# Start addresses of the large tiles in a decoder layer: multiples of 128 bytes, weight parts 64 bytes behind one

## The chip, the cores and the metric

One Trainium2 chip, of which the kernel uses one core. The metric is the device time of one execution in microseconds (us), the median of several runs. Lower is better.

## What is computed

One layer of a decoder over 256 tokens of width 1024, in float32, batch 1. Three steps add to the residual `x`, and a last RMSNorm follows.

```python
h = rmsnorm(x, norm_mix_g)
x = x + concat(conv_group(h), attention_group(h), gla_group(h)) @ w_out   # groups read columns of h @ w_in
h = rmsnorm(x, norm_xattn_g)
x = x + memory_cross_attention(h, rmsnorm(mem, norm_mem_g), wq, wkv, wo)  # 4 heads, 256 memory tokens
h = rmsnorm(x, norm_ffn_g)
u = causal_dwconv(h @ w_up)                                               # width 3, 2 x 2752 channels
a, g = split(u)
x = x + (silu(a) * g) @ w_down
return rmsnorm(x, final_norm_g)
```

The products must have nearly float32 precision. The kernel gets it from three products in the type float32r: a matrix is split into a high part (its rounding to float32r) and a low part (what is left), and high times high, high times low and low times high are summed in PSUM.

## The kernel before

**Weights.** All weights come from HBM as one stream of pieces of 128 x 1024 float32 (512 KB; some are narrower), in the order of `_stream_order`. `emit_load` (L112) lets SyncE fetch a piece into one of 6 raw tiles. `emit_split` (L128) makes the two parts of it: ScalarE copies the piece into `hi` as float32r (L152), and VectorE subtracts, `lo = raw - hi` (L159). Each part has a pool of 4 slots of 1024 elements (tags `high` and `low`, L146 and L147). Four pieces go to tiles that are idle at the time instead: the two of `wo` to the slot with tag `big`, the two of `up` pair 0 to the slot with tag `parts` (`SPARE`, L49, L136 to L141). `piece` (L164) keeps loads 6 and splits 2 or more pieces ahead of their use.

**Activations.** The moving side of most products is a normed and split activation: `xg` (tag `xg`), `y` (tag `parts`), `memg` and `hn` (tag `hn`), each 16 blocks of 128 x 256, 8 for the high and 8 for the low part. The FFN's hidden values (`hid`, 128 x 256 blocks for high and low of each of 21 channel groups and a tail) take the same three slots again, 16 blocks in each: first `big`, then `parts`, then `xg` (L779 to L782).

**Products and the order on TensorE.** A product with 256 moving columns holds a 128 x 128 block of weights as its stationary side and streams 256 tokens: `first` (L279, 144 matmuls), `in`, `xk`, `xq` and `up` (`feature_tile`, L203 to L212), `out` (`products`, L201), `wo` (L760), and `up` pair 0 (L850). In four places the weights are the moving side and a 128 x 128 block of activations is stationary: `gv` (L442, 272 columns), `v` (L458, 512 columns), `xv` (L718, 256 columns) and the down-projection `dn` (L887, L891, 512 columns, whose stationary side is `hid`). TensorE goes through these one after the other in the written order: `first`; `in` mixed with `gv`, `v` and the small products of the attention and gated groups; `xk`; `out`; `xq`, `xv` and the cross-attention; `wo`; `up` for pairs 0 to 20 and a tail; `dn`. Pairs 0 to 2 of `up` read `xg` and are scaled afterwards, later ones read `hn`, which GpSimd, ScalarE and VectorE make while pairs 1 and 2 run (L861, L187, L190). VectorE and ScalarE do the convolution and the gate of a pair (`activate`, L812) while TensorE is on the next.

**Where a tile starts.** A pool hands out bytes in the order in which its tags are first used, each rounded up to 32 bytes per partition. What starts behind a small or odd-sized tile (the residual with its 8 gains in front, `par` with 213 columns, `eps`, `one`, `lr1`) therefore starts at a multiple of 32, and not always of 128. The start of a slot modulo 128 bytes, as the built program has it:

| slot | holds | before | changed |
|---|---|---|---|
| `res` (2) | residual `x`, `x1`, `x2` | 0 and 32 (the values of `x` 32 further) | 0 and 0 (the values of `x` 0) |
| `big` | attention inputs, parts of `wo`, `hid` of groups 0 to 7 | 64 | 0 |
| `parts` | `y`, parts of `up` pair 0, `hid` of groups 8 to 15 | 0 | 0 |
| `xg` | `xg`, `hid` of groups 16 to 20 and the tail | 96 | 0 |
| `hn` | `memg`, `hn`, final output | 0 | 0 |
| `keep` | row norms | 96 | 0 |
| `high`, `low` (4 each), part used as stationary | weights of `first`, `in`, `xk`, `out`, `xq`, `up` | 0 | 64 |
| `high`, `low`, part used as moving | weights of `gv`, `v`, `xv`, `dn` | 0 | 0 |
| `big`, parts of `wo` | stationary | 64 | 64 |
| `parts`, parts of `up` pair 0 | stationary | 0 | 64 |

Blocks inside these tiles lie 512 or 1024 bytes apart, so a whole product has one pair of starts modulo 128 (`gv` has two: its weight blocks are 1088 bytes apart).

Of the kernel before, what the change touches and what calls it, by code (L numbers as in the profile page):

```python
# [10 lines left out]
F32 = mybir.dt.float32  # L11
BF16 = mybir.dt.bfloat16
F32R = mybir.dt.float32r
# [6 lines left out]
P = 128  # L20
T = 256
D = 1024
KT = D // P
# [13 lines left out]

PG_X, PG_MEM, PG_FFN = 0, 8, 16
P_SCW, P_SCB, P_GN, P_FW, P_FB = 32, 38, 40, 41, 170
NPARAM = 213  # L40

RAW, PARTS, AHEAD = 6, 4, 2
EARLY, STATS, MIXED, TURNED = 3, (1, 0), 1, 3
# [4 lines left out]

SPARE = {("wo", 0): "big", ("wo", 1): "big", ("up", 0, 0): "parts", ("up", 0, 1): "parts"}  # L49
SLOT = 1024  # L50

X_WITH = {1: (1, 2), 2: (2, 4), 4: (4, 8)}

# [16 lines left out]
def _width(key):  # L70
    return {"first": 768, "gla": 544}.get(key[0], 1024)
# [3 lines left out]
def trunk(ctx: ExitStack, tc: tile.TileContext, xT, x_rows, w_stream, params, gate, final, out):  # L75
# [3 lines left out]
    cp = ctx.enter_context(tc.tile_pool(name="cp", bufs=1))  # L79
    rp = ctx.enter_context(tc.tile_pool(name="rp", bufs=RAW))  # L80
    hp = ctx.enter_context(tc.tile_pool(name="hp", bufs=PARTS))
    t1p = ctx.enter_context(tc.tile_pool(name="t1p", bufs=16))
    t2p = ctx.enter_context(tc.tile_pool(name="t2p", bufs=11))
    smp = ctx.enter_context(tc.tile_pool(name="smp", bufs=12))
# [3 lines left out]
    def ps(name):  # L88
        banks["turn"] += 1
        return pp.tile([P, 512], F32, tag=banks["tags"][banks["turn"] % len(banks["tags"])], name=name)  # L90
# [4 lines left out]
    def t2(name):  # L95
        return t2p.tile([P, 2, T], F32, tag="t2", name=name)
# [8 lines left out]
    spare = {}  # L105
    state = {"load": 0, "split": 0, "until": place[("up", 0, 0)]}

    def load_x(k0, k1):
        a, b = (KT + k0 * T if k0 else 0), KT + k1 * T
        sp.dma_start(xt[:, a:b], xT[:, a:b])  # L110

    def emit_load():  # L112
        i = state["load"]
        state["load"] += 1
        key = order[i]
        t = rp.tile([P, SLOT], F32, tag="raw", name="w_" + "_".join(map(str, key)))
        if i == 0:

            act.dma_start(t[:, :384], w_stream[i, :, :384])
            load_x(0, 1)  # L120
            sp.dma_start(t[:, 384:768], w_stream[i, :, 384:768])
        else:
            if key[0] == "first" and key[1] in X_WITH:
                load_x(*X_WITH[key[1]])
            sp.dma_start(t[:, :_width(key)], w_stream[i, :, :_width(key)])
        raw[key] = t

    def emit_split(pin=False):  # L128
        i = state["split"]
        state["split"] += 1  # L130
        key = order[i]
        if key[0] == "mem":
            return
        n = _width(key)
        t = raw[key]
        if key in SPARE:  # L136
            tag = SPARE[key]
            if key[-1] == 0:
                spare[tag] = cp.tile([P, 16, T], F32R, tag=tag, name="spare_" + tag)
            view = lambda c: spare[tag][:, 8 * key[-1] + c:8 * key[-1] + c + 4, :].rearrange("p a b -> p (a b)")  # L140
            hi, lo = view(0), view(4)  # L141
        elif key[0] == "dtail":
            hi = cp.tile([P, n], F32R, name="h_dtail")
            lo = cp.tile([P, n], F32R, name="l_dtail")
        else:
            hi = hp.tile([P, SLOT], F32R, tag="high", name="h_" + "_".join(map(str, key)))[:, :n]  # L146
            lo = hp.tile([P, SLOT], F32R, tag="low", name="l_" + "_".join(map(str, key)))[:, :n]  # L147
        if i == 0:
            act.copy(hi[:, :384], t[:, :384])
            dve.tensor_copy(hi[:, 384:], t[:, 384:n])  # L150
        else:
            c = act.copy(hi, t[:, :n])  # L152
            if pin:
                tc.keep_in_program_order(c)
        if key[0] == "dtail":
            pool.memset(lo[TAIL:].bitcast(F32), 0.0)
            c = dve.tensor_sub(lo[:TAIL], t[:TAIL, :n], hi[:TAIL])
        else:
            c = dve.tensor_sub(lo, t[:, :n], hi)  # L159
        if pin:  # L160
            tc.keep_in_program_order(c)
        parts[key] = (hi, lo)
# [29 lines left out]
    def pair(t, n):  # L192

        return t[:, 0:n, :], t[:, n:2 * n, :]
# [16 lines left out]
            s, m = term(k)  # L211
            pe.matmul(dst, s[a], m[b], start=(n == 0), stop=(n == len(todo) - 1))  # L212

    xt = cp.tile([P, KT + KT * T], F32, tag="res", bufs=2, name="x")
    x = xt[:, KT:].rearrange("p (k n) -> p k n", k=KT)
    emit_load()
    act.preload_act_table_set("natural_log_exp_and_others")
    for _ in range(RAW - 1):
# [5 lines left out]
    for _ in range(KT - RAW):  # L224
        emit_load()
    par = cp.tile([P, NPARAM], F32, name="par")
    sp.dma_start(par, params)
# [6 lines left out]
    dve.memset(heat, 0.0)  # L234
    ones = cp.tile([P, P], F32, name="ones")
    dve.memset(ones, 1.0 / D)
    eps = cp.tile([P, 1], F32, name="eps")
    dve.memset(eps, EPS)
    one = cp.tile([P, 1], F32, name="one")
    dve.memset(one, 1.0)  # L240


# [87 lines left out]
    pool.memset(same, 0.0)  # L330
    for h in range(4):
        pool.memset(same[32 * h:32 * h + 32, 64 * (h % 2):64 * (h % 2) + 64], 1.0)
    lr1 = cp.tile([P, 2, 17], F32, name="lr1")
    pool.memset(lr1, 1.0)
    big = cp.tile([P, 16, T], F32, tag="big", name="mix")
    yt = cp.tile([P, 2 * KT, T], F32R, tag="parts", name="y")
# [81 lines left out]

    mgt = cp.tile([P, 2 * KT, T], F32R, tag="hn", name="memg")
    mg = pair(mgt, KT)  # L420
    macc = cp.tile([P, T], F32, name="m_acc")

    def memory(i):
        m = piece("mem", i)[:, :1024].rearrange("p (k n) -> p k n", k=4)
# [7 lines left out]


    gv = t2("gv")
    lrT = cp.tile([17, T], F32, name="lrT")
    gps = [ps("gv0"), ps("gv1")]
    for i in range(4):
        w = blocks(piece("gla", i), 272)
# [115 lines left out]
    for n, dst in ((0, ue[:, 0:P]), (2, ue[:, P:T]), (1, uo[:, 0:P])):  # L554
        a = 64 * (n % 2)
# [18 lines left out]
    for j in range(2):  # L574
        for h in range(4):
            a = 64 * (h % 2)
# [23 lines left out]
    for c in range(2):  # L600
# [9 lines left out]
        f = t1(f"yg{c}")  # L610
# [119 lines left out]
    for c in range(2):  # L730
        o = ps(f"xo{c}")
        for m in range(2):
            for h in (2 * c, 2 * c + 1):
                a = 64 * (h % 2)
# [93 lines left out]
    def second_root():  # L828
        spread(r2, diags2, "x2")

    r2, ready = smp.tile([P, T], F32, tag="r2", bufs=1, name="r2"), []
    for j in range(NPAIR + 1):
        tail = j == NPAIR
        src = []
        for t in range(1 if tail else 2):
# [6 lines left out]
            elif t == 1:  # L842
# [13 lines left out]
                _, diags2 = root_of(tot2, "x2")  # L856
                tc.keep_in_program_order(act.preload_act_table_set("silu_and_others"))
            if (j, t) == STATS:
                for k in range(KT):
                    f = t1(f"hn{k}")  # L860
# [5 lines left out]
        if j >= STATS[0]:  # L866
            for args in ready:
                activate(*args)
            ready = []
# [29 lines left out]
    k0 = NPAIR - LEAD  # L899
# [35 lines left out]
def _layout(inp):  # L935
    f = lambda n: np.asarray(inp[n], np.float32)
    actT = lambda a: _rows(a[0].T, KT).reshape(P, KT * T)
# [6 lines left out]
    down = w_down[:NPAIR * P].reshape(NPAIR, P, 2, 512).transpose(1, 2, 0, 3).reshape(P, 21, 1024)  # L944

    order = _stream_order()
    stream = np.zeros((len(order), P, SLOT), np.float32)
    for i, key in enumerate(order):
        kind, n = key[0], key[1] if len(key) > 1 else 0
        if kind == "first":  # L950
            a = w_first[n]
        elif kind == "in":
            a = _tile(w_in, n)
        elif kind == "mem":
            a = memT[:, 1024 * n:1024 * n + 1024]
        elif kind == "gla":
            a = _rows(w_gla[256 * n:256 * n + 256], 2)
        elif kind == "mv":
            a = _rows(w_in[256 * n:256 * n + 256, MV:MV + 512], 2)
        elif kind == "out":  # L960
            a = _tile(w_out, n * P)
        elif kind == "wq":
            a = _tile(wq, n * P)
        elif kind == "memk":
            a = _tile(wkv, n * P)
        elif kind == "memv":
            a = _rows(wkv[512 * n:512 * n + 512, 256:], 4)
        elif kind == "wo":
            a = wo.reshape(2, P, KT, P).transpose(1, 2, 0, 3)[:, 4 * n:4 * n + 4]
        elif kind == "up":  # L970
            a = _tile(w_up, n * P + key[2] * DFF)
        elif kind == "uptail":
            a = _tile(tail, 0)
        elif kind == "dtail":
            a = np.concatenate([w_down[NPAIR * P:]] * 2, 0)
        else:
            a = down[:, n]
        a = a.reshape(a.shape[0], -1)
        stream[i, :a.shape[0], :a.shape[1]] = a

    par = np.zeros((P, NPARAM), np.float32)
    for at, n in ((PG_X, "norm_xattn_g"), (PG_MEM, "norm_mem_g"), (PG_FFN, "norm_ffn_g")):
# [7 lines left out]
    for j in range(NPAIR + 1):  # L990
# [4 lines left out]
        for t, c in enumerate(chans):  # L995
            n = 2 * j + t
            par[:, P_FW + 3 * n:P_FW + 3 * n + 3] = cw[:, c].T
            par[:, P_FB + n] = cb[c]
    gate = np.concatenate([f("gla_w_gate")[0], f("gla_b_gate")], 0)
    xT = np.concatenate([f("norm_mix_g").reshape(KT, P).T, actT(f("x"))], 1)  # L1000
    final = np.tile(f("final_norm_g").reshape(1, D), (P, 1))
    return [np.ascontiguousarray(xT), np.ascontiguousarray(f("x")[0]), stream, par, np.ascontiguousarray(gate), final]

# [19 lines left out]
```

## Time and profile before

| what | value |
|---|---|
| median of 3 runs (lowest, highest) | 342.38 us (342.32, 342.47) |
| the profiled execution's own time | 342.1 us |
| its span, first to last instruction | 340.4 us |
| matmuls in the span | 2462 |
| TensorE busy | 331.5 us, 97% |
| TensorE weight loads busy | 306.6 us, 90% |
| VectorE, ScalarE busy | 258.0 us (76%), 210.8 us (62%) |
| mean granted clock of TensorE | 0.997 |

The span lies inside the profiled execution's time, which is 1.7 us longer; that execution is 0.3 us under the median. Busy time of an engine counts the stretches in which at least one of its instructions runs. Matmuls overlap in their pipeline, so how fast a product goes is read from the distance of the starts of its matmuls, not from the duration of one.

### The profile page before, as it was taken

The page shows a single profiled execution, that of the slowest core. Times are in us where ns is not written, and L with a number is a line of the kernel's source. Part 1 is how long each engine was busy: PE and PEld are TensorE (multiplying, and loading weights), DVE is VectorE, ACT ScalarE, POOL GpSimd, SP SyncE. Part 2 cuts the span into 40 slices and gives each one's busy share as a digit, 9 for nine tenths or more (in the row PEclk, how much of TensorE's full clock was granted, in tenths as well). Part 3 has the DMA queues.
Part 4 walks back from the last instruction along what each step waited for, and adds up shares of the span by engine and source line. Part 5 has one row for each costly group of instructions (what it writes and reads, how often), then busy time and mean ns, then how long its engine had stood idle before and what let it go on. Part 6 is the DMA issues. An engine that isn't in the chain of part 4 may idle for free.

```text
span 340.4 us, 6402 instructions
## 1 busy us (share of the span) xinstructions
PE 331.5 (97%) x2462; PEld 306.6 (90%) x2462; DVE 258.0 (76%) x486; ACT 210.8 (62%) x390; POOL 13.3 (4%) x32
## 2 busy tenths in 40 slices
PE   6999999999999999999999999999999999999992
PEld 3999879898999999899899999999999988888881
DVE  5978878797987858578999988888889874454411
ACT  3574999566666655586786666666667654353333
POOL 6000000000000000005400000000000000000000
PEclk9999999999999999999999999999999999999998
DMA  7989753743377534108238765555557546563003
GB/s 211 417 309 324 255 179 103 236 157 129 122 247 249 183 126 129 59 13 287 71 125 244 234 203 188 186 182 182 183 174 241 185 154 194 196 188 104 0 0 123
DMA packets 17888, 60.37 MB, mean 177 GB/s; under 512 B 1969, under 2 KB 2626, under 8 KB 17858
## 3 DMA queue, kind: packets, MB, share of 16 engines
q1 hardware_dynamic: 17426, 59.24, 52.1%
q10 hardware_dynamic: 432, 0.72, 0.6%
q8 instruction: 19, 0.31, 0.4%
q14 instruction: 11, 0.09, 0.1%
HBM read 58.91 MB, written 1.05 MB: 176 GB/s over the span
## 4 chain that ended last, share of the span: by engine, by line
PE 93%; ACT 3%; DVE 2%; DMA 1%; issue 0%; DVEq 0%
PE up L212 35%; PE dn L887 17%; PE in L212 10%; PE out L201 7%; PE first L279 5%; PE v L458 3%; PE gv L442 2%; PE xq L212 2%; PE xv L718 2%; PE wo L760 2%; PE xk L212 2%; ACT h_up L152 1%; DMA x<-in_xT_dram 1%; PE et L385 1%; ACT x_sq L752 1%; PE o L395 1%
## 5 line engine op out<-in xcount | busy, mean ns | idle before, releaser
L212 PE MATMUL up<-hn,h_up 128*128 128x256 f32 x576 | 76.6, 284 | 0.1
L212 PEld LDWEIGHTS up<-hn,h_up 128*128 128x128 f32 x576 | 72.1, 192 | 1.2 <-ACT hn L187 0.9
L152 ACT CAST h_up<-w_up 128x1024 fp32r<-128x1024 f32 x40 | 41.7, 1047 | 24.2 <-PE up L212 24.2
L159 DVE TENSOR_TENSOR l_up<-w_up,h_up 128x1024 fp32r<-128x1024 f32 x40 | 48.7, 1221 | 8.8 <-ACT h_up L152 8.7
L887 PE MATMUL dn<-h_down,hid 128*128 128x512 f32 x168 | 52.7, 392 | 0.0
L159 DVE TENSOR_TENSOR l_down<-w_down,h_down 128x1024 fp32r<-128x1024 f32 x21 | 25.7, 1226 | 25.9 <-ACT h_down L152 25.9
L212 PE MATMUL up<-hn,l_up 128*128 128x256 f32 x288 | 40.4, 283 | 0.0
L152 ACT CAST h_down<-w_down 128x1024 fp32r<-128x1024 f32 x21 | 22.1, 1051 | 29.1 <-PE dn L887 24.9
L887 PEld LDWEIGHTS dn<-h_down,hid 128*128 128x128 f32 x168 | 31.6, 188 | 6.9
L212 PEld LDWEIGHTS up<-hn,l_up 128*128 128x128 f32 x288 | 37.1, 192 | 0.0
L791 DVE SCALAR_TENSOR_TENSOR u<-up,par,u 128x255 f32<-128x255 f32 x74 | 35.1, 477 | 0.6
L887 PE MATMUL dn<-l_down,hid 128*128 128x512 f32 x84 | 32.9, 392 | 0.0
L212 PE MATMUL in<-xg,h_in 128*128 128x256 f32 x192 | 25.8, 286 | 0.0
L212 PEld LDWEIGHTS in<-xg,h_in 128*128 128x128 f32 x192 | 23.8, 188 | 0.7 <-issue 0.5
L789 ACT ACTIVATE u<-up,par 128x256 f32<-128x256 f32 x37 | 20.5, 555 | 0.0
L887 PEld LDWEIGHTS dn<-l_down,hid 128*128 128x128 f32 x84 | 15.8, 188 | 3.5
L201 PE MATMUL out<-y,h_out 128*128 128x256 f32 x128 | 16.7, 283 | 0.0
L201 PEld LDWEIGHTS out<-y,h_out 128*128 128x128 f32 x128 | 15.9, 192 | 0.0
L159 DVE TENSOR_TENSOR l_in<-w_in,h_in 128x1024 fp32r<-128x1024 f32 x12 | 14.6, 1220 | 1.0 <-ACT h_in L152 0.6
L152 ACT CAST h_in<-w_in 128x1024 fp32r<-128x1024 f32 x12 | 12.5, 1047 | 4.3 <-issue 2.8
L279 PE MATMUL first<-xg,h_first 128*128 128x256 f32 x96 | 13.2, 284 | 0.9 <-DVE h_first L150 0.5
L861 POOL TENSOR_TENSOR hn<-x,r 128x256 f32<-128x256 f32 x8 | 7.7, 1002 | 149.8 <-DVE r L313 149.8
(270 smaller groups left out, 561.1 us busy)
## 6 DMA issues: line engine op xcount, KB each, us to landing
w_up<-in_w_stream_dram SPq DMA_DIRECT2D x42, 512.0 KB, 3.4
w_down<-in_w_stream_dram SPq DMA_DIRECT2D x21, 512.0 KB, 3.3
w_in<-in_w_stream_dram SPq DMA_DIRECT2D x12, 512.0 KB, 4.4
w_out<-in_w_stream_dram SPq DMA_DIRECT2D x8, 512.0 KB, 3.4
w_first<-in_w_stream_dram SPq DMA_DIRECT2D x7, 384.0 KB, 8.1
w_mv<-in_w_stream_dram SPq DMA_DIRECT2D x4, 512.0 KB, 4.3
w_gla<-in_w_stream_dram SPq DMA_DIRECT2D x4, 272.0 KB, 4.1
xtok<-in_x_rows_dram SPq DMA_DIRECT2D x1, 1024.0 KB, 9.7
```

What stands on the lines that cost most here:

```text
L152: c = act.copy(hi, t[:, :n])
L159: c = dve.tensor_sub(lo, t[:, :n], hi)
L201: pe.matmul(dst, s, m, start=(n == 0), stop=(n == len(todo) - 1))
L212: pe.matmul(dst, s[a], m[b], start=(n == 0), stop=(n == len(todo) - 1))
L279: pe.matmul(fps[i][:, :T], w[a][:, i * P:(i + 1) * P], xg[b][:, k, :], start=(k == 0 and (a, b) == (0, 0)), stop=(k == KT - 1 and a == 1))
L442: pe.matmul(gps[j][:, :272], xg[a][:, 2 * i + k, j * P:(j + 1) * P], w[b][:, k, :], start=(i == 0 and k == 0 and (a, b) == (0, 0)), stop=( ...
L458: pe.matmul(vps[j], xg[a][:, 2 * i + k, j * P:(j + 1) * P], w[b][:, k, :], start=(i == 0 and k == 0 and (a, b) == (0, 0)), stop=(i == 3 an ...
L718: pe.matmul(vps[j][:, :T], mg[a][:, 4 * i + k, j * P:(j + 1) * P], w[b][:, k, :], start=(i == 0 and k == 0 and (a, b) == (0, 0)), stop=(i ...
L789: act.activation(v, src, AF.Identity, bias=fb(t), scale=fw(t, 2))
L791: dve.scalar_tensor_tensor(v[:, s:], src[:, :T - s], fw(t, 2 - s), v[:, s:], op0=ALU.mult, op1=ALU.add)
L861: pool.tensor_mul(f, x2[:, k, :], r2)
L887: pe.matmul(q, hid[i](k)[:, cols], w[j], start=False, stop=(k == NPAIR - 1 and i == 1), skip_group_check=True)
```

## The change

Nothing is added to or taken from what the engines compute. What changes is where tiles start:

- Tiles ahead of a large one are padded: the gains in front of `x` from 8 to 32 columns, `par` from 213 to 224, `eps` and `one` from 1 to 32, the last axis of `lr1` from 17 to 32. The inputs in HBM are padded alike, so the first transfer of `x` has 288 columns and not 264.
- A weight part that will be stationary begins `ASIDE` = 16 elements (64 bytes) into its slot, which is 32 elements longer; one that will be moving (`MOVING`) begins at the slot's start. The spare slots do the same.
- `m_acc`, `lrT` and `r2` (the row norm of the FFN) share one slot of 256 columns (tag `row`), which makes room for the padding.

```diff
-NPARAM = 213
+NPARAM = 224
...
+ASIDE = 16
+MOVING = ("gla", "mv", "memv", "down", "dtail")
+
+PADDED = 32
...
     def load_x(k0, k1):
-        a, b = (KT + k0 * T if k0 else 0), KT + k1 * T
+        a, b = (PADDED + k0 * T if k0 else 0), PADDED + k1 * T
         sp.dma_start(xt[:, a:b], xT[:, a:b])
...
             if key[-1] == 0:
-                spare[tag] = cp.tile([P, 16, T], F32R, tag=tag, name="spare_" + tag)
-            view = lambda c: spare[tag][:, 8 * key[-1] + c:8 * key[-1] + c + 4, :].rearrange("p a b -> p (a b)")
-            hi, lo = view(0), view(4)
+                spare[tag] = cp.tile([P, 4 * SLOT + 32], F32R, tag=tag, name="spare_" + tag)
+            view = lambda c: spare[tag][:, ASIDE + c * SLOT:ASIDE + (c + 1) * SLOT]
+            hi, lo = view(2 * key[-1]), view(2 * key[-1] + 1)
...
-            hi = hp.tile([P, SLOT], F32R, tag="high", name="h_" + "_".join(map(str, key)))[:, :n]
-            lo = hp.tile([P, SLOT], F32R, tag="low", name="l_" + "_".join(map(str, key)))[:, :n]
+            at0 = 0 if key[0] in MOVING else ASIDE
+            hi, lo = (hp.tile([P, SLOT + 32], F32R, tag=tag, name=tag[0] + "_" + "_".join(map(str, key)))[:, at0:at0 + n]
+                      for tag in ("high", "low"))
...
-    xt = cp.tile([P, KT + KT * T], F32, tag="res", bufs=2, name="x")
-    x = xt[:, KT:].rearrange("p (k n) -> p k n", k=KT)
+    xt = cp.tile([P, PADDED + KT * T], F32, tag="res", bufs=2, name="x")
+    x = xt[:, PADDED:].rearrange("p (k n) -> p k n", k=KT)
...
-    eps = cp.tile([P, 1], F32, name="eps")
+    eps = cp.tile([P, 32], F32, name="eps")[:, :1]
...
-    one = cp.tile([P, 1], F32, name="one")
+    one = cp.tile([P, 32], F32, name="one")[:, :1]
...
-    lr1 = cp.tile([P, 2, 17], F32, name="lr1")
+    lr1 = cp.tile([P, 2, 32], F32, name="lr1")[:, :, :17]
...
-    macc = cp.tile([P, T], F32, name="m_acc")
+    macc = cp.tile([P, T], F32, tag="row", name="m_acc")
...
-    lrT = cp.tile([17, T], F32, name="lrT")
+    lrT = cp.tile([P, T], F32, tag="row", name="lrT")[:17]
...
-    r2, ready = smp.tile([P, T], F32, tag="r2", bufs=1, name="r2"), []
+    r2, ready = cp.tile([P, T], F32, tag="row", name="r2"), []
```

The order of instructions stays as it was on TensorE, GpSimd and SyncE. One instruction moves: on ScalarE the first square of the memory tokens (`m_acc`). Before, it stands ahead of the gains of the memory tokens (`memg`) and of the gate (`lb`, which reads the product `z` of `lrT`):

```order
45 L387 COPY p_643<-et_639 128x384
46 L428 ACTIVATE m_acc<-w_mem_645 128x256
47 L187 ACTIVATE memg<-w_mem_645,par 128x256 x3
48 L152 CAST h_in_734<-w_in_611 128x1024
49 L474 ACTIVATE lb<-z 128x256
```

In the changed kernel, whose lines stand 7 further down, it stands behind them:

```order
45 L394 COPY p_643<-et_639 128x384
46 L194 ACTIVATE memg<-w_mem_645,par 128x256 x4
47 L159 CAST h_in_734<-w_in_611 128x1024
48 L481 ACTIVATE lb<-z 128x256
...
53 L435 ACTIVATE m_acc<-w_mem_645 128x256
```

So the square is written after `lrT`, whose slot it now takes, has been read by TensorE.

## Rows read from the trace of the kernel before

**Rows 1.** The page's parts 1 and 2: busy time, and 40 equal slices.

```profile
PE 331.5 (97%) x2462; PEld 306.6 (90%) x2462; DVE 258.0 (76%) x486; ACT 210.8 (62%) x390; POOL 13.3 (4%) x32
PE   6999999999999999999999999999999999999992
PEclk9999999999999999999999999999999999999998
```

**Rows 2.** The page's part 4: the chain that ended last, by engine.

```profile
PE 93%; ACT 3%; DVE 2%; DMA 1%; issue 0%; DVEq 0%
```

**Rows 3.** Chain in short windows, 256-column products, weights at 0: start us, us, what.

```profile
12.43 10.68 PE first L279 x89
24.38 5.16 PE in L212 x43
99.95 21.12 PE out L201 x176
156.98 8.04 PE up L212 x67
174.95 95.16 PE up L212 x793
```

**Rows 4.** The same view inside `wo`: 256 columns, weights at 64, `xo` at 0.

```profile
141.27 5.30 PE wo L760 x45
```

**Rows 5.** The same view inside the down-projection: hid in big, parts, xg.

```profile
274.89 10.30 PE dn L887 x45
285.89 10.21 PE dn L887 x45
296.79 4.92 PE dn L887 x21
```

**Rows 6.** The same view inside `v` (512 columns) and `gv` (272 columns).

```profile
42.89 1.64 PE v L458 x7
31.96 5.16 PE gv L442 x41
```

**Rows 7.** Waits: engine line waited for: us in total, times, longest us.

```profile
ACT h_down L152 <- PE dn L887: 24.9, 16, 1.8
ACT h_up L152 <- PE up L212: 24.2, 26, 1.2
PE first L279 <- DVE l_first L159: 0.6, 1, 0.6
PEld up L212 <- ACT hn L187: 0.9, 4, 0.2
```

**Rows 8.** Stretches: us, busy us (instructions) of PE PEld DVE ACT POOL, clock, DMA.

```profile
166.00:275.00 109.00, 108.93 (x895) 107.68 (x895) 98.06 (x169) 74.85 (x125) 0.00 (x0) 1.00 0.59 191
275.00:335.00 60.00, 59.39 (x259) 48.26 (x257) 26.17 (x29) 24.82 (x35) 0.00 (x0) 1.00 0.36 120
335.00:341.00 6.00, 0.00 (x0) 0.00 (x0) 0.88 (x2) 1.52 (x6) 0.00 (x0) 0.79 0.23 87
```

**Rows 9.** The split of a piece, page part 5: busy, mean ns of one, idle before.

```profile
L152 ACT CAST h_up<-w_up 128x1024 fp32r<-128x1024 f32 x40 | 41.7, 1047 | 24.2 <-PE up L212 24.2
L159 DVE TENSOR_TENSOR l_up<-w_up,h_up 128x1024 fp32r<-128x1024 f32 x40 | 48.7, 1221 | 8.8 <-ACT h_up L152 8.7
```

**Rows 10.** The same for the parts of `wo`, written at 64: duration min/median/max.

```profile
L152 ACT CAST spare_big<-w_wo x2: 1046/1048/1050, 87.4 to 100.0; 128x1024 fp32r<-128x1024 f32 x2
L159 DVE TENSOR_TENSOR spare_big<-w_wo,spare_big x2: 1219/1222/1226, 95.7 to 101.1; 128x1024 fp32r<-128x1024 f32 x2
```

**Rows 11.** DMA issues at the start: KB each, us to landing.

```profile
w_first<-in_w_stream_dram ACTq DMA_DIRECT2D x1, 192.0 KB, 3.5
x<-in_xT_dram SPq DMA_DIRECT2D x1, 132.0 KB, 3.3
```

**Rows 12.** Users of `m_acc` and `lrT`: duration min/median/max, first and last start.

```profile
L428 ACT ACTIVATE m_acc<-w_mem x1: 412/412/412, 43.3 to 43.3; 128x256 f32<-128x256 f32 x1
L288 PE MATMUL m_ms<-m_acc,ones x2: 379/379/379, 92.6 to 92.8; 128*128 128x256 f32 x2
L472 PE MATMUL z<-wg,lrT x4: 270/270/372, 44.7 to 45.1; 17*128 17x128 f32 x4
```

**Rows 13.** GpSimd's part of `hn`: duration min/median/max, first and last start.

```profile
L861 POOL TENSOR_TENSOR hn<-x,r x8: 742/920/1749, 157.4 to 164.2; 128x256 f32<-128x256 f32 x8
```

**Rows 14.** Timeline of TensorE from the first product with `hn`: start us, us, instructions.

```profile
166.29 3.75 PE L212 MATMUL up<-hn,h_up 128*128 128x256 f32 x16
```

More of the change, by code (lines that the diff above doesn't have):

```diff
@@ L999, in _layout @@
     gate = np.concatenate([f("gla_w_gate")[0], f("gla_b_gate")], 0)
-    xT = np.concatenate([f("norm_mix_g").reshape(KT, P).T, actT(f("x"))], 1)
+    xT = np.concatenate([f("norm_mix_g").reshape(KT, P).T, np.zeros((P, PADDED - KT), np.float32), actT(f("x"))], 1)
     final = np.tile(f("final_norm_g").reshape(1, D), (P, 1))
```

## Prediction

> **What bounds the kernel now.** I read the busy shares first. TensorE has work for 97% of the span, and from the second of the 40 slices to the last but one its row shows nines, at the full granted clock of 2.4 GHz [rows 1]. The chain that ended last says the same: 93% of it is TensorE [rows 2]. The next engine, VectorE, is busy 98.06 of 109 us in the long up-projection and 26.17 of 60 us in the down-projection [rows 8]. Where it and ScalarE idle over a piece of weights, they wait for TensorE to give a slot back (24.2 and 24.9 us) [rows 7]. So the end is set by how close the matmuls follow each other, and a nanosecond on each of 2000 of them is 2 us.
>
> Hence the distance between starts. A piece of the chain that holds only back-to-back matmuls gives it: its length divided by its count. For 256 columns and weights at a multiple of 128 bytes it is 120.0 ns everywhere: `first` 10.68 / 89, `in` 5.16 / 43, `out` 21.12 / 176, `up` 8.04 / 67 with `xg` and 95.16 / 793 with `hn` [rows 3]. The 256 columns alone take 256 / 2.4 = 106.7 ns, so 13.3 ns of each is something else.
>
> Now the point on which all rests: the same instruction runs at different distances where only start addresses differ. In the down-projection (512 columns, moving weights at 0) it is 10.30 / 45 = 228.9 ns with `hid` at 64, 10.21 / 45 = 226.9 ns with `hid` at 0 and 4.92 / 21 = 234.3 ns with `hid` at 96 [rows 5]. The product `v`, whose stationary `xg` is also at 96, has 1.64 / 7 = 234.3 ns too [rows 6]. At 256 columns the moving side's start alone does nothing (`xg` at 96 and `hn` or `y` at 0 both give 120.0 ns [rows 3]). But one product already has what the change gives to all: in `wo` the weights are at 64 and the moving `xo` at 0, and there it is 5.30 / 45 = 117.8 ns [rows 4]. So 120.0 - 117.8 = 2.2 ns.
>
> The Trainium skill speaks against this: "SBUF — State Buffer", section "SBUF: two separate sides", says that TensorE has its own ports and never waits on anyone, which leaves no room for a start address; by it the sum is zero and the time stays 342.4 us. The rows of the down-projection disagree, with up to 7.4 ns between starts.
>
> **The change part by part.**
>
> 1. *256 columns, weights from 0 to 64.* These are `first` 144, `in` 288, `xk` 48, `out` 192, `xq` 48, and `up` 48 + 96 + 888: 1752 matmuls. `wo` and `xv` keep their starts. At 2.2 ns that is 3.85 us. Two stretches cannot keep it. The first 55 matmuls of `first` come before 12.43 us and partly wait for VectorE's split (0.6 us [rows 7]). And the some 77 matmuls of `up` between 156.98 us and the first with `hn` at 166.29 us [rows 3, 14] run while GpSimd makes `hn`, eight multiplications of 742 to 1749 ns in a row until 165 us [rows 13]. The first 16 with `hn` take 3.75 us [rows 14] where 16 starts and a tail are about 2.1, so `hn` is what is late there, and what TensorE gains ahead of it is waited away. That leaves 1752 - 55 - 77 = 1620, so **-3.56 us**. Bounds: nothing, if `wo` owes its pace to something else; at the far end 13.3 ns each, 21.5 us, if all that a matmul takes beyond its columns came from where its sides start. No row of this form has less than 11.1 ns beyond them (`wo`), so I count on 2.2 and, for the range, on at most a quarter more, 4.5 us. A loss is priced under the rivals.
>
> 2. *512 columns, stationary to 0.* `dn` with `hid` in `xg`: 68 matmuls from 234.3 to 226.9, 0.50 us. `v`: 48 by the same 7.4 ns, 0.36 us. `dn` with `hid` in `big`: 96 matmuls from 228.9 to 226.9, 0.19 us. Together **-1.05 us**. The target value is measured on the same instruction in the slot `parts`, which stays at 0. Its bounds are narrow: from 0.7 to 1.2 us.
>
> 3. *`gv`*: 272 columns, 5.16 / 41 = 125.9 ns with `xg` at 96 [rows 6]. That is already 12.5 ns over 272 / 2.4 = 113.3, less than the 13.3 ns of the other rows. No row has its new pair of starts. I take nothing; 48 matmuls by 6 ns either way are 0.3 us, kept for the range.
>
> 4. *The split.* Both halves now write 64 bytes into a slot. Written at 64, the parts of `wo` took 1048 and 1222 ns [rows 10]; at 0 those of `up` took 1047 and 1221 ns [rows 9]. Nothing, then. If it did cost a little, the cover is the wait of 24.2 us on slots that TensorE has not yet left [rows 7].
>
> 5. *The first transfer of `x`* grows from 132 to 144 KB. Between the two transfers shown, 60 KB more take 0.2 us more [rows 11], so 12 KB are **+0.04 us**, and it lies on the path, since the first split waits for it. By the whole 3.3 us over 132 KB it would be 0.3 us; zero if a transfer's latency covers it. The rest of `x` and `par` come later and are not waited for.
>
> 6. *The shared slot.* `m_acc` was written at 43.3 us and is read by TensorE at 92.6 us; `lrT` is read until about 45.5 us [rows 12]. The square moves behind that read on ScalarE. With 47 us until its reader it costs nothing, and the gains of the memory tokens that stand behind it come a square earlier. `r2` is written after 156 us, when `m_acc` is long dead.
>
> 7. *Strided fill of `lr1`* on GpSimd: under 0.2 us, 30 us ahead of its use. Nothing.
>
> Sum: -3.56 - 1.05 + 0.04 = -4.57 us. The profiled execution took 342.1 us and would take 337.5. It lies 0.3 us under the median of 342.4, so the median becomes **337.8 us**. VectorE keeps up: in `up` it has 109.00 - 98.06 = 10.9 us left [rows 8], and the stretch loses about 2 us. The last 5 us, where TensorE is done [rows 8], stay.
>
> **The rivals.**
>
> *Only some slots gain.* The parts of `wo` start 192 bytes past a multiple of 256; the four `high` and the four `low` slots are now 4224 bytes apart, so they start by turns 64 and 192 past one. If the pattern repeats every 256 bytes and not every 128, half of the pieces pass at 117.8 and the others at 120.0. For it: no row shows 64. Against it I have no row either: the blocks inside a tile lie 512 bytes apart, which fits both periods. Time: half of 3.56 is 1.78, so 342.4 - 1.78 - 1.05 + 0.04 = 339.6 us.
>
> *Only the 512-column part comes.* The 120.0 ns would be a pace of its own that 256 columns fall into, and `wo`'s 117.8 one of its short stretch between transpositions. For it: `xg` at 96 and `hn` at 0 have exactly the same 120.0 ns. Against: 45 starts in a row keep the 117.8. Time: 342.4 - 1.05 + 0.04 = 341.4 us.
>
> *Slower.* In the down-projection a stationary side at 64 is not better but worse than one at 0, 228.9 against 226.9 ns [rows 5]. If the weights of the 256-column products behave like that with `xg`, `hn` and `y`, each of the 1752 matmuls costs 2.0 ns more: +3.50 - 1.05 + 0.04 gives 344.9 us. It decides from an average of 120.0 + 1.01 / 1752 us = 120.6 ns on. For it: the rows at 512 columns. Against: the only row at 256 columns with 64 bytes between the sides goes the other way.
>
> *Nothing changes.* Start addresses would not reach TensorE, the differences in the down-projection would come from the stage (its loads, its neighbours), and the time stays 342.4 us. Against it: `v`, at 43 us, repeats the 234.3 ns of the down-projection at 297 us, with the same start and nothing else in common. The Trainium skill's rule on ports, quoted above, would have it so.
>
> **How the numbers follow.** The forecast 0.62, some slots 0.17, 512 columns alone 0.08, nothing 0.05, slower 0.08. A measurement of this kernel can tell 0.2%, 0.7 us, from no change. So faster is 0.62 + 0.17 + 0.08 = 0.87, the same 0.05, slower 0.08. The predicted time is that of the likeliest case. Its lower end takes the 4.5 us of part 1 (another 0.9) and the 0.3 of `gv`: 336.6. The upper end goes past the second case by some 0.8 for `gv`, the first transfer and the loose times of GpSimd [rows 13]: 340.4. That holds the first two cases, 0.79 of the chance.
>
> **What would show it.** In the changed profile the pieces of chain in `out` and `up` should have 117.8 ns a matmul (the 888 matmuls of `up` with `hn` some 1.9 us shorter in all), the down-projection 226.9 ns in all three thirds, `v` 226.9. Parts 4 and 5 keep their durations. The stall at the first product with `hn` grows by about 0.2 us. I am wrong if `out` stays at 120.0 (then the third case), if `out` and `up` change pace from piece to piece (the second), or if it is above 120.6 (the fourth).

## The result and the profile after

| | before | changed |
|---|---|---|
| median (lowest, highest), 4 runs each on one chip | 342.43 us (342.32, 342.55) | 333.43 us (333.21, 333.53) |
| ratio, 95% interval | | 0.9728 (0.9714 to 0.9742) |
| the profiled execution, its span | 342.1 us, 340.4 us | 333.4 us, 331.6 us |
| TensorE's mean granted clock | 0.997 | 0.995 |

The change gains 9.0 us. The forecast was 4.6 us, and its range ended at 336.6 us: the direction is right, the size is half of what came. First the page of the changed kernel: busy time by engine (part 1), and the chain that ended last, by engine (part 4).

```profile
PE 322.4 (97%) x2462; PEld 296.7 (89%) x2462; DVE 257.6 (78%) x486; ACT 210.9 (64%) x390; POOL 13.3 (4%) x32
...
PE 87%; ACT 4%; DMA 4%; DVE 2%; POOLq 1%; SPq 1%; issue 0%; POOL 0%
```

As many instructions as before, and TensorE busy for 9.1 us less of a span that is 8.8 us shorter; VectorE's and ScalarE's busy time is the same to 0.4 us [rows 1]. So the time came from TensorE's own pace. The chain in short windows shows where (start us, length us, what); length by count is the distance between starts:

```profile
24.19 4.88 PE in L219 x42
97.89 7.66 PE out L208 x65
105.90 13.15 PE out L208 x116
138.38 4.71 PE wo L767 x40
169.89 92.14 PE up L219 x813
46.89 1.63 PE v L465 x7
31.94 4.12 PE gv L449 x33
265.78 10.34 PE dn L894 x45
276.81 10.36 PE dn L894 x45
287.87 4.36 PE dn L894 x19
```

A 256-column product now has two paces (a pace is the distance between the starts of successive matmuls). `out` begins at 7.66 / 65 = 117.8 ns and then runs at 13.15 / 116 = 113.4 ns; `up` has 92.14 / 813 = 113.3 ns where it had 120.0 [rows 3]; `in` is at 116.2 ns, a mixture. `wo`, which the change leaves alone, still has 4.71 / 40 = 117.8 ns [rows 4]. `gv` is at 124.8 ns (125.9 before [rows 6]). At 512 columns a stretch of `v` has 232.9 ns where it had 234.3, and the down-projection has 229.8, 230.2 and 229.5 ns in its three thirds, where it had 228.9, 226.9 and 234.3 [rows 5]: the middle third got slower.

The sums of the distances between starts, product by product, in us:

| | before | changed | difference | forecast |
|---|---|---|---|---|
| `first` | 18.93 | 18.88 | -0.05 | -0.20 |
| `in` | 35.97 | 34.73 | -1.24 | -0.63 |
| `xk` | 5.84 | 5.53 | -0.31 | -0.11 |
| `out` | 23.04 | 22.08 | -0.96 | -0.42 |
| `xq` | 6.04 | 5.80 | -0.24 | -0.11 |
| `wo`, `xv` | 11.88 | 11.85 | -0.03 | 0 |
| `up` | 126.04 | 120.28 | -5.76 | -2.10 |
| `v` | 11.77 | 11.63 | -0.14 | -0.36 |
| `dn` | 59.49 | 59.64 | +0.15 | -0.69 |

The forecast column is the prediction's 2.2 ns by its own counts (in `first` 144 - 55 = 89 matmuls, in `up` 1032 - 77 = 955), and its part 2 for `v` and `dn`. At 256 columns the direction is right and the size too small by a factor of 2 to 3, but for `first`, which gained less than forecast. At 512 columns less came than forecast, and for `dn` a loss.

The split of a piece (part 5 of the page) writes 64 bytes into a slot at the same speed as at 0 [rows 9]; in the waits ScalarE now waits less for slots, and in the stretch of `up` VectorE fills more of a shorter time (us, then busy us and instructions of PE, PEld, DVE, ACT, POOL, clock, DMA):

```profile
L166 DVE TENSOR_TENSOR l_up<-w_up,h_up 128x1024 fp32r<-128x1024 f32 x40 | 48.6, 1219 | 4.6 <-ACT h_up L159 3.7
L159 ACT CAST h_up<-w_up 128x1024 fp32r<-128x1024 f32 x40 | 41.5, 1045 | 14.3 <-PE up L219 14.1
```

```profile
ACT h_up L159 <- PE up L219: 14.1, 17, 1.2
```

```profile
162.00:265.00 103.00, 102.85 (x891) 101.34 (x890) 97.30 (x169) 74.73 (x126) 0.00 (x0) 1.00 0.61 199
```

ScalarE's wait on slots fell from 24.2 [rows 7] to 14.1 us, and VectorE's free time in `up` from 10.9 us of 109 [rows 8] to 103.00 - 97.30 = 5.7 us of 103. That is the cover left for the next such gain.

### The profile page after: what moved, and what is told of

Its sections match the earlier page's. It is cut to its first block, busy times and chain, and to the rows that moved or that the text cites. A ratio compares the mean times of both kernels' runs of the same rounds, so it can differ in the third digit from the quotient of the medians.

```text
span 331.6 us, 6402 instructions
## 1 busy us (share of the span) xinstructions
PE 322.4 (97%) x2462; PEld 296.7 (89%) x2462; DVE 257.6 (78%) x486; ACT 210.9 (64%) x390; POOL 13.3 (4%) x32
## 4 chain that ended last, share of the span: by engine, by line
PE 87%; ACT 4%; DMA 4%; DVE 2%; POOLq 1%; SPq 1%; issue 0%; POOL 0%
PE up L219 31%; PE dn L894 17%; PE in L219 10%; PE out L208 7%; PE v L465 3%; DMA xtok<-in_x_rows_dram 3%; PE gv L449 2%; PE xv L725 2%; PE wo L767 2%; PE xq L219 2%; PE xk L219 2%; PE first L286 1%; ACT h_up L159 1%; DVE u L798 1%; DMA w_first<-in_w_stream_dram 1%; PE et L392 1%
## 5 line engine op out<-in xcount | busy, mean ns | idle before, releaser
L219 PE MATMUL up<-hn,h_up 128*128 128x256 f32 x576 | 73.3, 278 | 0.1
L219 PEld LDWEIGHTS up<-hn,h_up 128*128 128x128 f32 x576 | 68.6, 188 | 1.7 <-ACT hn L194 1.3
L159 ACT CAST h_up<-w_up 128x1024 fp32r<-128x1024 f32 x40 | 41.5, 1045 | 14.3 <-PE up L219 14.1
L219 PE MATMUL up<-hn,l_up 128*128 128x256 f32 x288 | 38.5, 276 | 0.0
L219 PEld LDWEIGHTS up<-hn,l_up 128*128 128x128 f32 x288 | 35.4, 188 | 0.0
L219 PE MATMUL in<-xg,h_in 128*128 128x256 f32 x192 | 25.1, 283 | 0.0
L219 PEld LDWEIGHTS in<-xg,h_in 128*128 128x128 f32 x192 | 23.1, 188 | 0.7 <-issue 0.5
L208 PE MATMUL out<-y,h_out 128*128 128x256 f32 x128 | 16.0, 277 | 0.0
```

The source lines that it names most:

```text
L208: pe.matmul(dst, s, m, start=(n == 0), stop=(n == len(todo) - 1))
```

## The experiments

Theory 1: what counts is the distance between the starts of the two sides, modulo 128 bytes; 64 is good. Its rivals: the start of the weights alone counts (theory 2), or the multiples of 128 of all other tiles (theory 3). All edits are to the changed kernel unless another is named. A time is the median of 4 to 7 runs up to e10 (of 2 in e7 and e8), with the ratio to the kernel before and its 95% interval; from e11 on it is a single run.

**The 64 bytes taken back (e1).**

```diff
-ASIDE = 16
+ASIDE = 0
```

> The changed kernel with ASIDE = 0: every large tile still begins at a multiple of 128 bytes, but the stationary weights do too. Theory 1 (what counts at 256 columns is how far the start of the stationary side lies from that of the moving side, modulo 128 bytes; 64 apart lets a product settle at 113.3 ns, 0 apart holds it at 120.0): out, xk and up go back to 120.0 ns, time 341 to 342.5 us. Rival, theory 3 (the alignment of all the other tiles brings the gain): out and up stay at 113 to 115 ns, time 333 to 335 us.

341.09 us, ratio to before 0.996 (0.9947 to 0.9973). The chain:

```profile
102.89 15.14 PE out L208 x127
169.62 92.38 PE up L219 x773
```

119.2 and 119.5 ns. The 64 bytes bring 341.09 - 333.43 = 7.7 us; theory 3 falls. The rest of the change brings 1.3 us, and not by padding alone: the lengthened slots start by turns 0 and 128 bytes past a multiple of 256, and so do the weights in them. The chain of `up` inside a piece at 128 and inside the next one at 0:

```profile
205.28 2.61 PE up L219 x22
208.00 2.64 PE up L219 x22
```

118.6 ns at 128 and 120.0 ns at 0: the 119.2 and 119.5 are averages of two slots.

**The 64 bytes alone (e2).** The kernel before with `ASIDE`, `MOVING` and the shared slot, without the paddings, so that `xg` stays at 96.

> The kernel before with the weights' 64 bytes alone (and the shared slot that makes room): xg stays at 96, hid at 64, 0 and 96, hn and y at 0. Theory 1: out, xk and up with hn settle at 113.3 ns, which is 6.6 us of the 9.0; first, in, xq and up with xg, whose sides are now 32 apart, go at some pace between 113.3 and 120.0; time 333.5 to 337 us. Theory 2 (the weights' own start counts, whatever the moving side's): all 256-column products at 113 to 118 ns, xg's too. Theory 3: 341 to 343 us.

335.0 us, ratio 0.9782 (0.9759 to 0.9805).

```profile
84.92 4.13 PE in L217 x35
102.98 15.12 PE out L206 x132
169.89 92.14 PE up L217 x813
```

`up` with `hn` at 0 has its 113.3 ns and `out` with `y` at 0 its 114.5, both at 64 bytes from their weights. `in`, whose weights now lie 32 bytes ahead of `xg` at 96 (modulo 128), has 118.0 ns. The start of the weights alone is not enough: theory 2 falls, and theory 1 holds so far. One expectation of it failed: `xk`, with 64 bytes between its sides, was to settle at 113.3 ns and stayed at 117.7 for its 48 matmuls.

**Other distances (e3, e4, e8).** `ASIDE` = 8, 32 and 20 elements: 32, 128 and 80 bytes.

> The changed kernel with ASIDE = 8, weights 32 bytes behind a multiple of 128. Theory 1: a pace between those of 0 and 64 bytes in out and up, 113.3 to 120.0 ns, time 333 to 342 us; if only the exact distance of 64 helps, 120.0 ns and 342 us.

> The changed kernel with ASIDE = 32, weights 128 bytes further than in the kernel with ASIDE = 0. If the pattern repeats every 128 bytes, this is that kernel again: 120.0 ns in out and up, 341 to 342.5 us. If it repeats every 256 bytes, it is not: the slots' starts only change places (0 and 128 past a multiple of 256), so the pieces would change pace by turns in both kernels, and a pace other than 120.0 shows in either.

> The changed kernel with ASIDE = 20, weights 80 bytes behind. If only a distance near 64 bytes lets a product settle, and 80 is near enough, out and up run at 113.3 ns and the time is 333 to 334 us; if it needs 64 exactly, they run at 117 to 119 ns as with 32 bytes, 339 to 341 us.

341.09 us (0.9957, 0.9943 to 0.9971), 341.01 us (0.996, 0.9943 to 0.9978) and 338.89 us (0.9889, 0.9856 to 0.9923). `up` in e3, e4 and e8, one fence each:

```profile
169.99 92.11 PE up L219 x773
```

```profile
169.91 92.12 PE up L219 x773
```

```profile
170.00 92.09 PE up L219 x782
```

119.2, 119.2 and 117.8 ns, each again an average of two slots 128 bytes apart modulo 256. e4 is e1 with the slots' places exchanged, hence the same average: 120.0 ns at 0 and 118.3 at 128 in `out`. In e8 the slots have 118.9 ns at 80 and 116.7 at 208. So the distance counts modulo 256, and theory 1 has its period wrong; only at 64 and 192 are the two slots alike, at 113.3 in the long run. Of the distances tried, only these two give it.

**512 columns (e5, e6).** In the changed kernel the slots of moving weights start by turns 0 and 128 bytes past a multiple of 256, and `hid` always 128 past. e5 puts the moving weights of `v` and `dn` (but the FFN's tail) 128 past, e6 all of them at 0; in e6 the last line of the edit has `32 * odd`.

```diff
-            at0 = 0 if key[0] in MOVING else ASIDE
+            odd = (key[-1] + (key[0] == "down")) % 2 if key[0] in MOVING else 0
+            at0 = 32 * (1 - odd) if key[0] in MOVING else ASIDE
```

> The changed kernel, but weights that move begin 128 bytes into every second slot, so that they and the stationary hid lie at the same start modulo 256 bytes (128 past a multiple). Theory D (at 512 columns the pattern repeats every 256 bytes: the same start gives 227 ns, 128 apart 233 to 234): dn runs at 226.7 to 228 ns throughout and takes 0.6 us less, v the same, time 332.5 to 333.0 us. Rival (dn's pace changes by turns for another reason, its slots or the stage): dn stays at 230.3 ns on average, 333.4 us.

> The opposite: the weights that move always begin at a multiple of 256 bytes, 128 from hid. Theory D: dn at 232.6 to 234 ns throughout, 0.6 us more, 334.0 us. Rival: 230.3 ns and 333.4 us.

332.6 us (0.9705, 0.9683 to 0.9726) and 333.93 us (0.9752, 0.9723 to 0.978). The chain in the first two thirds of `dn`, e5 and then e6:

```profile
265.94 10.20 PE dn L895 x45
276.82 10.20 PE dn L895 x45
```

```profile
265.83 10.22 PE dn L895 x44
276.99 10.22 PE dn L895 x44
```

226.7 ns with equal starts modulo 256, 232.3 with 128 between them; the changed kernel's 230 is the mean of the two. So at 512 columns, too, the distance counts modulo 256, and 0 is the best of those that ran. Before, `hid` in `parts` met every slot at 0 modulo 256, hence the 226.9 of [rows 5]. `v` stays at 230.1 ns in e5; why, is open.

**The order of the products (e7).** `wo` takes its three products block by block, `up` the whole tile's one kind after the other. e7 gives `up` the order of `wo`.

```diff
-        todo = [(k, a, b) for g in (ks, late) for a, b in ((0, 0), (0, 1), (1, 0)) for k in g]
+        todo = [(k, a, b) for g in (ks, late) for k in g for a, b in ((0, 0), (0, 1), (1, 0))]
```

> The changed kernel with the matmuls of in, xk, xq and up in the order that wo and up pair 0 have (block by block, the three products of a block together). Theory S (a product starts at 117.8 ns and settles at 113.3 after a small disturbance; wo and up pair 0 are too short or not disturbed): up with hn still settles at 113.3 ns, time within 0.7 us of 333.4. Rival O (the order of wo holds it at 117.8): up stays at 117.8 ns, 888 x 4.5 ns = 4 us more and some 2 us in the other products, 337 to 340 us.

333.02 us (0.9718, 0.9685 to 0.9751).

```profile
170.29 91.75 PE up L219 x807
```

113.7 ns: the order is not what keeps `wo` at 117.8.

**A version that beats both (e9).** e5 with equal starts for `mv` and `down` alone, the blocks of `gla` padded from 272 to 288 columns, the moving weights of `gv` and `xv` 64 bytes from their activations, and one part of the FFN's tail shifted by 128.

> The kernel of the run with equal starts (dn and v at 128 past a multiple of 256 on both sides), and in addition gv and xv with their moving weights 64 bytes from the stationary side (gv's blocks padded from 272 to 288 columns so that all of them are), and the moving weights of the FFN's tail shifted like the others where the slot allows it. Theory 1 holds for weights that move, too: xv falls from 119 to between 113.3 and 118 ns, gv from 125 to between 120 and 123, together 0.3 to 0.6 us less than 332.6: 332.0 to 332.4 us. Rival (only a stationary side 64 behind helps): xv and gv as before, 332.6 us.

332.33 us (0.9696, 0.9675 to 0.9717), 10.2 us under the kernel before as timed with it (342.53); against e5 the 0.3 us lie within the intervals. `xv` falls from 119 to 116 ns a product, `gv` does not move.

**A cut product (e10).** e9, with one product near the start of `out` and of both stretches of `up` pair 0 issued as two of 128 columns, to see whether such a break throws a product into the fast pace.

> The same kernel with one matmul cut into two of 128 columns near the start of out and of both stretches of up pair 0, as a deliberate disturbance. Theory S (a product at 117.8 ns settles at 113.3 once it is disturbed): out, which ran its first 72 matmuls at 117.8 ns, is at 113.3 from the cut on, 0.3 us less for about 0.1 to 0.2 us of cost, time 331.8 to 332.3 us. Rival (settling depends on something else): out keeps 117.8 ns for its first tiles, time 0.2 us above the run without the cuts.

332.99 us (0.972, 0.9687 to 0.9752), not better than e9. Behind the cuts both halves of pair 0 ran at 113 ns (36 of its matmuls at 114 ns or less, none in e9). For the first half this says little: it does so without a cut in e5, e6, e7, e11 and e18 (21 of its 24 matmuls); the second half does it in no other run. `out` reached 113 ns with its second tile, not its fourth:

```profile
100.95 18.13 PE out L216 x160
```

That is 113.3 ns. But `up` with `xg` fell into its pace later, and `first`, which comes ahead of every cut, took 0.55 us more than in e9, so the time cannot be put down to the cuts. Inconclusive: a break may start the fast pace, not every one does.

**Why `wo` stays at 117.8 ns (e11 to e18).** The forecast rested on this row. e11 and e12 issue the first twelve products of `wo` thirteen times over, in the changed kernel and in the kernel before; e13 and e14 add a cut in that row; e15 makes a cut in `out` of the kernel before.

```diff
-    def wo_part(o, k):
+    def wo_part(o, k, more=0):
...
-        for a, b in ((0, 0), (0, 1), (1, 0)):
-            pe.matmul(wps[o][:, :T], wb[a][:, 2 * (o % 4) + k, :], xo[b][:, k, :], start=(k == 0 and a + b == 0),
-                      stop=(k == 1 and a == 1))
+        for r in range(more, -1, -1):
+            for a, b in ((0, 0), (0, 1), (1, 0)):
+                pe.matmul(wps[o][:, :T], wb[a][:, 2 * (o % 4) + k, :], xo[b][:, k, :], start=(k == 0 and a + b == 0),
+                          stop=(a == 1 and (k == 1 or r > 0)))
...
-        wo_part(o, 0)
+        wo_part(o, 0, 12)
```

> The changed kernel, in which the first twelve products of `wo` are issued thirteen times over, each time from zero, so that 144 more 256-column matmuls stand in one row, with the same operands (weights at 64, `xo` at 0). Theory L: `wo` keeps 117.8 ns only because its row is too short; then the row falls to 113.3 ns within 40 to 100 matmuls and the time is 333.4 + 144 x 0.1133 to 0.1153 = 349.7 to 350.0 us. Theory W: something in `wo` (its slot, its `xo`, its order of blocks) keeps it at 117.8 ns however long it lasts; then all of the row has 117.8 ns and the time is 333.4 + 17.0 = 350.4 us.

> The same 144 matmuls more in the kernel before, whose `wo` has the same starts. Theory L: here too the row falls from 117.8 to 113.3 ns, in a kernel without one of the change's paddings, and the rows of before could have shown 113.3 if `wo` had been longer; time 342.4 + 16.3 to 16.6 = 358.7 to 359.0 us. Theory W: 117.8 ns throughout, 342.4 + 17.0 = 359.4 us.

> The changed kernel with the lengthened `wo` of e11, in whose row one product of 256 columns (the 53rd of 192) is issued as two of 128 columns. Theory P: at 64 bytes between the sides two repeating patterns are possible, 117.8 and 113.3 ns, and a row stays in the one it is in until something shifts it; then `wo` has 117.8 ns ahead of the cut and 113.3 behind it, about 135 x 4.5 = 0.6 us less than e11: 349.7 us. Theory Q: it is the operands of `wo` that hold it at 117.8; then 117.8 ns behind the cut too, 350.3 us.

> The kernel before with the same longer `wo` and the same cut. Theory P: 117.8 ns ahead of the cut and 113.3 behind it, in a kernel without any of the change's paddings: 358.7 us. Theory Q: 117.8 throughout, 359.3 us.

> The kernel before with one product near the start of `out` issued as two of 128 columns (weights and moving side both at 0). Theory P with a distance of 0: only one pace exists there, 120.0 ns ahead of the cut and behind it, and the time is that of the kernel before, within 0.3 us. If instead 120.0 is only an unshifted state that any start address could leave, `out` falls below 118 ns behind the cut and the kernel gains up to 1 us.

350.29, 359.31, 350.29 and 360.64 us; e15 342.47 beside 342.50 us. e14 missed its time: its row of `wo` is as in e12, but `first` had ended 1.2 us later. The chain inside the longer `wo` of e11 and e12, behind the cut in e13 and e14, and in `out` of e15, one fence each:

```profile
140.00 18.02 PE wo L768 x153
```

```profile
143.98 18.14 PE wo L761 x154
```

```profile
145.89 14.13 PE wo L772 x120
```

```profile
149.91 15.31 PE wo L765 x130
```

```profile
100.92 18.12 PE out L208 x151
```

117.8 ns four times: neither length nor this cut frees `wo`. Theory L falls, and of theory P the part that a cut shifts the pattern; that there are two paces and that a row keeps the one it is in stands. At a distance of 0 the cut in `out` changes nothing either (120.0 ns).

e16 puts 144 matmuls on the tiles of `wo` ahead of it, in one sum that is thrown away, over all eight blocks of weights and both blocks of `xo`; e17 starts a new sum every third matmul; e18 is e16 with the weights of `wo` in the slots `high` and `low` like those of `up`.

```diff
             wps[o] = ps(f"wo{o}")
+        if o + k == 0:
+            for n in range(144):
+                a, b = ((0, 0), (0, 1), (1, 0))[n % 3]
+                pe.matmul(wps[o][:, :T], wb[a][:, n // 3 % 8, :], xo[b][:, n // 3 % 2, :], start=(n == 0), stop=(n == 143))
...
-SPARE = {("wo", 0): "big", ("wo", 1): "big", ("up", 0, 0): "parts", ("up", 0, 1): "parts"}
+SPARE = {("up", 0, 0): "parts", ("up", 0, 1): "parts"}
```

The last two lines are of e18 alone; e17 has `start=(n % 3 == 0), stop=(n % 3 == 2)`.

> The changed kernel with 144 matmuls more ahead of `wo`, on the tiles of `wo`, but in the manner of `up`: one sum (one start, one end), the block of weights and of `xo` changing every third matmul; the sum is thrown away. Theory S: the frequent start of a new sum (every third matmul in `wo`, every 24th in `out` and `up`) holds `wo` at 117.8 ns; then this row falls to 113.3, 16.4 us more than the changed kernel. Theory T: where the tiles of `wo` lie holds it; then 117.8 ns throughout and 17.0 us more.

> The same 144 matmuls, but a new sum every third one. Theory S: 117.8 ns throughout, 17.0 us more than the changed kernel. If both this and the row with one sum fall to 113.3, it was the standing still on one block of `xo` in the longer `wo` of before that held it; if neither does, theory T.

> The row of 144 matmuls of e16 once more, but with the weights of `wo` in the slots `high` and `low`, as those of `up`, and not in `big`; their start stays 64 bytes behind a multiple of 128 and `xo` at one. If it is the place of the stationary tile that held `wo` at 117.8 ns, the row falls to 113.3 within 40 to 100 matmuls; if it is the place of `xo`, or something else in this stage, it stays at 117.8 to the end. The time tells nothing here, since the splits of `up` now wait for slots that `wo` holds.

350.12, 350.62 and 352.28 us. The chain inside the row, e16, e17 and e18:

```profile
139.98 15.31 PE wo L769 x130
```

```profile
139.94 15.66 PE wo L769 x133
```

```profile
141.15 14.85 PE wo L769 x131
```

117.8 and 117.7 ns, and then 14.85 / 131 = 113.4 ns. So theory S of e16 falls: neither the many sums nor the standing still on one block holds `wo` at 117.8. The row of e18 does not fall to 113.4 in its course, as was expected: it has it from its ninth start on, and the 48 products of `wo` proper keep it.

It would be rash to read from this that the place of the weights decides. By the built programs e18 differs from e16 in more than the place: the weights lie 64 bytes behind `xo` modulo 256 and not 192, and their high and low parts further apart. And the slots `high` and `low` are no warrant of the fast pace. In the same run `up` goes slowly for 96 matmuls, and 24 of them have their weights in the very slots that held those of the row (`high` at byte 0x27fc0 of the partition), 64 bytes behind `hn`. The chain over the 96 and inside the 24:

```profile
185.97 11.31 PE up L219 x96
189.04 2.59 PE up L219 x22
```

117.8 and 117.7 ns. So the place alone does not decide. What the traces do show appears when the start of each matmul is set beside the start addresses in the built programs, for the 12 runs in which most products have 64 bytes between their sides. Call a piece the matmuls that follow each other without a pause on the weights of one slot. Of 921 pieces none leaves the pace in which it has settled. Without a pause a product falls from 117.8 to 113.4 ns 47 times, each time at the step from a slot 192 bytes behind the moving side, modulo 256, to one 64 behind it. Such a step leaves it at 117.8 another 16 times; the 34 steps of other kinds within a product always do. Back to 117.8 without a pause it goes only at the step from `xk` to `out`, 10 times. After a pause it starts in either pace.

`wo` has no step that could free it: both its pieces lie in `big`, 192 behind `xo`, and with these starts it began at 117.8 in every run. `xk` in e2 has none either. This regularity was found in finished traces and no run tested it; by which mechanism it comes, and what decides the pace at a start, is open.

## Why the prediction was wrong, point by point

**What bounds the kernel: right.** TensorE sets the end, the distance between starts is the quantity to read, and addresses alone change it. e1 takes 7.7 of the 9.0 us back with one number. The rival that nothing changes fell: the pace went from 120.0 to 113.3 ns by start addresses alone. The sentence of the Trainium skill that stood behind it ("SBUF — State Buffer", section "SBUF: two separate sides": TensorE never waits on anyone) is about engines that contend with each other. It does not speak of the start addresses of TensorE's own operands, so what failed is what the prediction drew from it.

**Term 1, the step "120.0 - 117.8 = 2.2 ns", failed.** The mechanism was right, the price was not: most of the matmuls save 120.0 - 113.3 = 6.7 ns. The price came from `wo`, the one row of before with the new pair of starts. With this pair a product has two paces, and `wo` goes at the slower one: it starts in it in every run with its weights in `big` at these starts, and has none of the steps between slots at which the others leave it. Of the 1848 matmuls of 256 columns, 1417 now follow at 114 ns or less. Most of the rest have about 117.8: `wo`, pair 0 of `up`, the first three tiles of `out` and several of `in`; `xv`, whose weights move, stays at 119. The sums over these products fell by 8.6 us instead of 3.56. The range allowed a quarter more than 2.2 ns, on the ground that no row had less than 11.1 ns beyond its columns; one row is no floor. The 6.7 ns lie about halfway between the 2.2 and the 13.3 named as the far end.

**`first` gained nothing, and the reason given was incomplete.** Of its 144 matmuls 89 were to keep the gain, at the real 6.7 ns some 0.6 us; the sum fell by 0.05 us. The timelines of ScalarE and of TensorE in the changed kernel (start us, us, instructions) show what takes the larger part:

```profile
17.50 1.04 ACT L324 ACTIVATE xtok<-xtok 128x1024 f32<-128x1024 f32 x1
18.54 1.55 ACT L159 CAST h_first<-w_first 128x768 fp32r<-128x768 f32 x2
```

```profile
18.45 0.84 PE L286 MATMUL first<-xg,l_first 128*128 128x256 f32 x6
19.41 0.84 PE L286 MATMUL first<-xg,h_first 128*128 128x256 f32 x5
```

The last pieces of `first` are split behind the squares of `xtok`, whose transfer lands at 16.4 us (16.3 before), so TensorE waits for the split until 19.41 us. Two distances of 385 and 222 ns in place of 113 cost 0.38 us there. I had looked for such a wait only ahead of 12.43 us. There the first 55 matmuls took 8.41 us and not 8.24: a wait for the first split was longer (1.03 us between two starts, 0.74 before).

**The stall at `hn`: right in kind.** 0.2 us more were forecast; 0.49 came for the same 16 matmuls:

```profile
162.69 4.24 PE L219 MATMUL up<-hn,h_up 128*128 128x256 f32 x16
```

against 3.75 us [rows 14]. With TensorE faster by more than thought, GpSimd's eight multiplications are later by more.

**Term 2 failed.** The step was "the target value is measured on the same instruction in the slot `parts`, which stays at 0": 226.9 ns. The slot stays at 0 modulo 128; but the pattern at 512 columns repeats every 256 bytes (e5, e6), and the lengthened slots and the padding moved half of the pairs to 128 modulo 256. `dn` became 0.15 us longer instead of 0.69 shorter, and `v` fell by 0.14 us, not 0.36. These two take 1.06 us from the gain, while term 1 adds 5.0 to it. I had named the period of 256 as a rival for the 256-column products, where at 64 and 192 bytes both slots settle at 113.3 ns, and not for these.

**Terms 3 to 7: nothing against them.** `gv` became 1.1 ns a matmul faster, 0.05 us in all; the split kept its durations; nothing is seen of the shared slot. The 0.04 us of the first transfer of `x` do not show: it landed after 3.1 us, where it took 3.3 [rows 11].

**The rivals.** Half of the slots gaining, 512 columns alone, slower, and no change: none came. The first had a true part: a period of 256 there is, at 0 and 128 bytes (e1) and at 512 columns, but 64 and 192 settle at the same pace. 335.0 us in e2, with the 64 bytes alone, is already below the range.

## What to carry to other kernels

Where TensorE is the bound, divide the length of a back-to-back stretch by its count, product by product, and lay beside it the start addresses of both sides. In these runs the weights as stationary side 64 bytes from the moving side modulo 128 were best at 256 columns (113.3 ns in the long run, against 120.0 at 0), equal starts modulo 256 at 512 columns (226.7 against 232.3). Divide piece by piece: an average over slots with different starts hid the period of 256 in e1 and e4. And a price taken from one row holds for what that row shares with the others: a far end that only one row contradicts belongs into the range.

## What was unexpected of the hardware

At 64 bytes the same instruction has two steady paces. In `out` it changes from 117.8 to 113.4 ns in mid-stretch, with nothing waited for, and stays there. The change stands at a step from one slot of weights to the next, as all 47 changes of this kind do in these traces, from 192 to 64 bytes behind the moving side. In `wo`, with its weights in `big` and no such step, 117.8 ns held over more than 150 matmuls and across a cut (e11, e13). The same slots of weights at the same distance went at 113.4 ns in the row of e18 and at 117.8 in its `up`. What decides the pace in which a stretch starts, whether a break can set it (the second half of pair 0 in e10 against e13), and by which mechanism, no run shows. That `gv` (272 columns) is indifferent to its distance, and `v` stays at 230 ns with equal starts, is open as well.
